# Operands of matmuls at multiples of 512 bytes from each other, and the inverse root spread by fp32r hi and lo products

## Chip, cores, metric

The kernel runs on one core of one Trainium2 chip. The metric is the device time of one execution in microseconds (us), here the median of three runs. TensorE is called PE, VectorE DVE, ScalarE ACT, GpSimd POOL; PEld stands for PE's weight loads, which overlap its matmuls.

## The reference

A trunk of two layers over 1024 tokens of width 1024, in fp32. Layer 0 mixes tokens by one projection that feeds stick-breaking attention (8 heads of 64) and a gated linear recurrence (4 heads of 128), and one output projection; layer 1 by a convolution module (gated projection, causal depthwise convolution of 31 taps, layer norm, projection). After each follows an MLP with squared ReLU, and each part has an RMS norm ahead and a residual.

```
for layer in range(DEPTH):
    u = rmsnorm(h, norm_mix_g[layer])
    if layer % 2 == 0:
        h = h + parallel_ab_mixer(u, w_in_ab[j], w_out_ab[j], lower_bounds[layer], hg_norm_g[j])
    else:
        h = h + conformer_conv(u, conv_w_glu[j], ...)
    u = rmsnorm(h, norm_ffn_g[layer])
    h = h + squared_relu_mlp(u, w_ff1[layer], w_ff2[layer])
return rmsnorm(h, final_norm_g)
```

## The kernel before

**Tiling.** Activations lie transposed, 128 channels on the partitions, and the tokens are worked in two halves of H = 512. A projection loops over panels of 128 output channels. `panel` loads one panel of weights (512 KB) over the SP queue into `wraw` and splits it into fp32r parts, `whl`: hi on ACT (line 99), lo on DVE (line 100). `gemm` (lines 110 to 112) then runs, for each 128 channels of the input, three matmuls: hi by hi, hi by lo, lo by hi. The panel's 128x128 block is the stationary operand, which PE loads ahead of each matmul, and the input (128x512, hi or lo) is the moving one. The input is split in the same way: tiles `u` (normed input), `ou` (output of the mixer), `cu` (convolution) and `hid` (hidden layer of the MLP). An MLP pass of one half does 8 hidden panels from `u`, then 8 output panels from these 8 `hid`, four times over; at the end of the kernel the last 8 output panels are done for 256 tokens at a time, four of their panels kept in `w2` tiles.

**Places in memory.** Pools lie one behind the other in a partition, and a tile's place is the sum of what stands ahead of it. Worked out from the built program, modulo 512 bytes: `wraw`, `whl`, `u`, `ou`, `cu` and `hx` lie at 96; the tiles of the working pool `wk` (attention and recurrence) at 128 (`kl`, `vn`), 192 (`raw`, `kd`, `qs`, `ke`, most `vh`) or 0 (`wt`, `kn`, one `vh`). The hidden layer of the first MLP pass takes tiles of the pool `up`, as `u` does, at 96. When attention is done its pool is closed, and from then on `hid` tiles come from a pool `hid` of their own, at 288. The MLP's gemms then write PSUM tiles `mm2`, those from `u` and those from `hid` alike.

**The inverse root.** `stats` turns sums of squares into 1/sqrt, for 4 (at the very end 2) blocks of 128 tokens: `st` matmuls against ones (line 121), a scale on DVE (line 124, `st_m`), a power on POOL (line 126, `st_r`), one Newton step in three DVE steps (lines 128 to 130), and `stb` matmuls (line 133), which spread each column of `st_r` over all partitions by a product with the identity, both in fp32. ACT copies the result out (line 135). It is called 21 times.

**Order.** A scheduler with a timeline of its own places the instructions of each engine; `tc.high_priority` moves the lines under it forward. The layer-0 mixer (to about 655 us) interleaves projection panels with attention and recurrence by hand-written spans; after that PE runs gemms almost alone.

Of the kernel before, what the change touches and what calls it, by code (L numbers as in the profile page):

```python
# [8 lines left out]
F32 = mybir.dt.float32  # L9
F32R = mybir.dt.float32r  # L10
BF16 = mybir.dt.bfloat16
AF = mybir.ActivationFunctionType
ALU = mybir.AluOpType
PSUM = bass.MemoryType.PSUM

P = 128
D = 1024
T = 1024
H = 512
# [34 lines left out]
def kernel(  # L54
# [13 lines left out]
    PE, ACT, DVE, POOL = nc.tensor, nc.scalar, nc.vector, nc.gpsimd  # L68

    const = ctx.enter_context(tc.tile_pool(name="const", bufs=1))  # L70
# [3 lines left out]
    tp = ctx.enter_context(tc.tile_pool(name="tp", bufs=2))  # L74
# [4 lines left out]
    nc.scalar.dma_start(vec, vecs)  # L79
    ident = const.tile([P, P], F32, name="ident")  # L80
    make_identity(nc, ident)
    ones = const.tile([P, P], F32, name="ones")
    DVE.memset(ones, 1.0)
    nhalf = const.tile([P, 4], F32, name="nhalf")
    POOL.memset(nhalf, -0.5)

    o_dram = [tc.dram_tile([P, T], F32, name=f"o_dram{i}") for i in range(KT)]

# [25 lines left out]
    def stats(pool, tag, src, count, eps, dst):  # L114

        n = dst.shape[-1] // P
        with tc.high_priority(offset=SPRIO):
            ps = pool.tile([P, H], F32, tag=tag, name="st")
            for c in range(n):
                for i, x in enumerate(src):  # L120
                    PE.matmul(ps[:, 2 * c:2 * c + 2], x[:, c * P:(c + 1) * P], ones[:, 0:2],  # L121
                              start=i == 0, stop=i == len(src) - 1, skip_group_check=True)
            m = tp.tile([P, 4], F32, tag="st_m", name="st_m")[:, :n]
            DVE.tensor_scalar(m, ps[:, 0:2 * n:2], 1.0 / count, eps, ALU.mult, ALU.add)
            r = tp.tile([P, 4], F32, tag="st_r", name="st_r")[:, :n]
            POOL.tensor_tensor(r, m, nhalf[:, :n], ALU.pow)
            t = tp.tile([P, 4], F32, tag="st_t", name="st_t")[:, :n]
            DVE.tensor_tensor(t, r, r, ALU.mult)
            DVE.scalar_tensor_tensor(t, t, -0.5, m, ALU.mult, ALU.mult)
            DVE.scalar_tensor_tensor(r, t, 1.5, r, ALU.add, ALU.mult)  # L130
            pb = pool.tile([P, H], F32, tag=tag, name="stb")
            for c in range(n):
                PE.matmul(pb[:, c * P:(c + 1) * P], r[:, c:c + 1].broadcast_to([P, P]), ident,  # L133
                          start=True, stop=True, skip_group_check=True)
            ACT.activation(dst, pb[:, :n * P], AF.Copy)

    def colsum_sq(src, w=H, order=range(KT), two=False):

        acc = tp.tile([P, H], F32, tag="acc", name="acc", bufs=1)[:, :w]
        for i, k in enumerate(order):  # L140
            x = src(k)
            if i == 0:
                ACT.activation(acc, x, AF.Square)
            else:
                sq = tp.tile([P, H], F32, tag="sq", name="sq")[:, :w]
                ACT.activation(sq, x, AF.Square)
                if not two or i < KT - 1:
                    DVE.tensor_tensor(acc, acc, sq, ALU.add)
        return [acc, sq] if two else [acc]

    def split(t, x):

        ACT.activation(t[:, 0], x, AF.Copy)
        DVE.tensor_tensor(t[:, 1], x, t[:, 0].bitcast(F32), ALU.subtract)  # L154

    def utile(name):
        return up.tile([P, 2, H], F32R, tag="u", name=name)

    def parts(ts):
        return [(t[:, 0], t[:, 1]) for t in ts]  # L160
# [13 lines left out]


    s1 = ctx.enter_context(ExitStack())
    wk = s1.enter_context(tc.tile_pool(name="wk", bufs=1))
    pz = s1.enter_context(tc.tile_pool(name="pz", bufs=2, space=PSUM))


# [34 lines left out]
    rm0 = wk.tile([P, H], F32, tag="rm0", name="rm0")  # L215
    with tc.high_priority(offset=PRIO):
        stats(pz, "tr", colsum_sq(lambda k: xs[0][k], two=True), D, 1e-6, rm0)

    def norm1():

        rm1 = wk.tile([P, H], F32, tag="ot", name="rm1", bufs=2)
        stats(pz, "tr", colsum_sq(lambda k: xs[1][k], two=True), D, 1e-6, rm1)
        u0[1] = scaled(lambda k: xs[1][k], V_MIX, rm1)
# [2 lines left out]
    lg = vec[:, V_LB:V_LB + 12].rearrange("p (r h) -> p r h", r=3)  # L226
    lb = const.tile([P, 4], F32, name="lb")
    lbc = const.tile([P, 4], F32, name="lbc")
    mx = wk.tile([P, 4], F32, name="lbmx")
    ex = wk.tile([P, 3, 4], F32, name="lbex")  # L230
    DVE.tensor_tensor(mx, lg[:, 0], lg[:, 1], ALU.max)
    DVE.tensor_tensor(mx, mx, lg[:, 2], ALU.max)
    for r in range(3):
# [46 lines left out]

    kl = [wk.tile([P, T], F32R, name=f"kl{h}") for h in range(2)]
    POOL.memset(kl[0][64:128].bitcast(F32), 0.0)
    POOL.memset(kl[1][0:64].bitcast(F32), 0.0)
    qs, kd, vn, vh, vl = {}, {}, {}, {}, {}
# [139 lines left out]
    def hg(hd, hf, dst):  # L427
# [95 lines left out]
        def output():  # L523
            qd, iv, before = hin[hd, "q", hf], hin[hd, "i", hf], L["before"]
            av = pz.tile([P, 4, P], F32, tag="av", name="ho")
            for c in range(4):
                PE.matmul(av[:, c], iv[:, c], L["sT"][:, c], start=True, stop=before[c] is None)
                if before[c] is not None:
                    PE.matmul(av[:, c], before[c], qd[:, c * P:(c + 1) * P], start=False, stop=True)
            L["av"] = av.rearrange("p c q -> p (c q)")  # L530
            sq = tp.tile([P, H], F32, tag="sq", name="hsq")
            ACT.activation(sq, L["av"], AF.Square)
            L["rh"] = wk.tile([P, H], F32, tag="ot", name="hrh", bufs=2)
            stats(pz, "tr", [sq], P, 1e-6, L["rh"])
# [73 lines left out]
    def rt():  # L608
        return late[0].tile([P, H], F32, tag="rbc", name="rbc", bufs=2)
# [75 lines left out]
    for name in TOKENS.split():  # L685
        f, n = name[0], name[1:]
# [14 lines left out]
        else:  # L701
            f, n, hf = name[:-2], int(name[-2]), "ab".index(name[-1])
# [53 lines left out]
    def ln_silu(ys):  # L756
        acc = tp.tile([P, H], F32, tag="acc", name="lacc", bufs=1)
        DVE.tensor_tensor(acc, ys[0], ys[1], ALU.add)
        for c in range(2, KT):
            DVE.tensor_tensor(acc, acc, ys[c], ALU.add)  # L760
        ps = pm2.tile([P, H], F32, tag="st", name="mean")
        PE.matmul(ps, ones, acc, start=True, stop=True)
        mu = tp.tile([P, H], F32, tag="sq", name="mu")
        ACT.activation(mu, ps, AF.Copy, scale=1.0 / D)
        for c in range(KT):
            DVE.tensor_tensor(ys[c], ys[c], mu, ALU.subtract)
        r = rt()
        stats(pm2, "st", colsum_sq(lambda c: ys[c]), D, 1e-5, r)
        res = []
        for c in range(KT):  # L770
            DVE.tensor_tensor(ys[c], ys[c], r, ALU.mult)
            DVE.tensor_scalar(ys[c], ys[c], vec[:, V_LNG + c:V_LNG + c + 1],
                              vec[:, V_LNB + c:V_LNB + c + 1], ALU.mult, ALU.add)
            sg = tp.tile([P, H], F32, tag="sq", name="sg")
            ACT.activation(sg, ys[c], AF.Sigmoid)
            DVE.tensor_tensor(sg, ys[c], sg, ALU.mult)
            res.append(utile("cu"))
            split(res[c], sg)
        return parts(res)
# [43 lines left out]
    steps(m, 8)  # L823
    ys = glu_conv(0, ug, m, 0)
    cu = ln_silu(ys)
    steps(m)
    ug = norm(1, V_MIX + 8)
    pw(cu, 0)
    ua = mlp_norm(1, 0)
    m = mlp(1, 0, ua)  # L830
    ys = glu_conv(1, ug, m, 3)
    cu = ln_silu(ys)
    steps(m, 24)
    pw(cu, 1)
# [66 lines left out]
```

## Time and profile before

| what | value |
|---|---|
| median of 3 runs | 2318.27 us (2317.86 to 2318.32) |
| profiled execution | 2317.94 us, its span 2316.2 us |
| PE busy | 2287.0 us (99%), 10828 matmuls |
| PEld, DVE, ACT, POOL busy | 1901.5, 1508.4, 884.9, 77.4 us |
| mean granted TensorE clock | 0.994 |

Busy time counts an instruction from its start to its end, and matmuls overlap; the pace of PE is read from starts. [...]

### The profile page before, as it was taken

Reading aid. Unit: us, or ns where it says so; the run is one execution under the profiler, and the core shown is the slowest. Engines: PE = TensorE matmul, PEld = TensorE weight load, DVE = VectorE, ACT = ScalarE, POOL = GpSimd, SP = SyncE. Lnnn points to the kernel's source line nnn. Section 1 sums busy time; section 2 is a strip of 40 time slices with the busy share of each in tenths; the row PEclk is TensorE's granted clock in tenths of the full one; section 3 lists DMA queues with packets and bytes.
Section 4 is the critical chain, followed back from the end, with each engine's and each line's share of the span. In section 5 each row is a group of like instructions: output and inputs, shape, how many; then the busy total and the mean of one; then the engine's idle time right before and its main releaser. Section 6 shows DMA issues by size and latency. Waiting matters only on the chain.

```text
span 2316.2 us, 27425 instructions
## 1 busy us (share of the span) xinstructions
PE 2287.0 (99%) x10828; PEld 1901.5 (82%) x10828; DVE 1508.4 (65%) x2156; ACT 884.9 (38%) x1338; POOL 77.4 (3%) x145
## 2 busy tenths in 40 slices
PE   8999999999999999999999999999999999999998
PEld 7888887788888888888888888888888888888888
DVE  7777777657443443469999866799997546333344
ACT  6444344434342333342414353341424534342341
POOL 1110000100000000000000000000000000000000
PEclk9999999999999999999999999999999999999999
DMA  4221122232333333323332322232322323323241
GB/s 171 69 67 44 49 69 62 89 125 86 111 128 103 94 98 95 96 91 96 96 98 93 96 95 91 91 100 91 100 91 91 100 97 104 117 91 100 91 137 46
DMA packets 67345, 217.97 MB, mean 94 GB/s; under 512 B 7696, under 2 KB 9872, under 8 KB 67216
## 3 DMA queue, kind: packets, MB, share of 16 engines
q1 hardware_dynamic: 55296, 197.16, 26.6%
q10 hardware_dynamic: 10640, 16.96, 2.3%
q0 software_dynamic: 1280, 2.10, 0.5%
q8 instruction: 85, 1.39, 0.2%
q14 instruction: 44, 0.36, 0.0%
HBM read 205.70 MB, written 8.39 MB: 92 GB/s over the span
## 4 chain that ended last, share of the span: by engine, by line
PE 93%; issue 3%; DVE 2%; DMA 1%; POOL 0%; ACT 0%; POOLq 0%; DVEq 0%; ACTq 0%
PE mm L110 26%; PE mm L111 26%; PE mm L112 26%; PE av L374 1%; PE pa L110 1%; PE pg L111 1%; PE pg L110 1%; PE pa L111 1%; PE pa L112 1%; PE pg L112 1%; PE wtr L365 1%; PE zs L466 1%; PE stb L133 1%; PE st L121 1%; PE z L345 1%
## 5 line engine op out<-in xcount | busy, mean ns | idle before, releaser
L100 DVE TENSOR_TENSOR whl<-wraw,whl 128x1024 fp32r<-128x1024 f32 x364 | 445.5, 1224 | 325.3 <-ACT whl L99 324.4
L99 ACT ACTIVATE whl<-wraw 128x1024 fp32r<-128x1024 f32 x364 | 384.5, 1057 | 695.8 <-PE mm L112 548.2
L110 PE MATMUL mm<-u,whl 128*128 128x512 f32 x1456 | 572.7, 394 | 8.3 <-ACT u L212 7.0
L111 PE MATMUL mm<-u,whl 128*128 128x512 f32 x1456 | 571.6, 393 | 1.4 <-DVE u L154 0.8
L112 PE MATMUL mm<-u,whl 128*128 128x512 f32 x1456 | 570.8, 392 | 0.0
L110 PE MATMUL mm<-hid,whl 128*128 128x512 f32 (+1 forms) x1024 | 396.8, 388 | 0.0
L111 PE MATMUL mm<-hid,whl 128*128 128x512 f32 (+1 forms) x1024 | 396.3, 387 | 0.0
L112 PE MATMUL mm<-hid,whl 128*128 128x512 f32 (+1 forms) x1024 | 396.1, 387 | 0.0
L753 DVE SCALAR_TENSOR_TENSOR y<-a,vec,y 128x512 f32<-128x512 f32 x480 | 345.0, 748 | 4.2
L110 PEld LDWEIGHTS mm<-u,whl 128*128 128x128 f32 x1456 | 274.0, 188 | 64.2 <-ACT u L212 7.0
L111 PEld LDWEIGHTS mm<-u,whl 128*128 128x128 f32 x1456 | 273.9, 188 | 56.1 <-DVE u L213 1.0
L112 PEld LDWEIGHTS mm<-u,whl 128*128 128x128 f32 x1456 | 274.0, 188 | 55.2 <-issue 0.2
L112 PEld LDWEIGHTS mm<-hid,whl 128*128 128x128 f32 x1024 | 191.9, 187 | 43.8
L111 PEld LDWEIGHTS mm<-hid,whl 128*128 128x128 f32 x1024 | 191.8, 187 | 43.7 <-issue 0.2
L110 PEld LDWEIGHTS mm<-hid,whl 128*128 128x128 f32 x1024 | 191.8, 187 | 43.5 <-issue 0.2
L654 DVE TENSOR_TENSOR ht<-ht,mm 128x512 f32<-128x512 f32 x120 | 82.5, 688 | 216.0 <-PE mm L112 215.6
L636 ACT ACTIVATE relu<-mm 128x512 f32<-128x512 f32 x128 | 76.5, 598 | 340.1 <-PE mm L112 331.6
L352 DVE TENSOR_TENSOR_SCAN ke<-ke 128x128 f32<-128x128 f32 (+5 forms) x64 | 86.3, 1352 | 23.6 <-POOL ke L349 23.0
L639 DVE TENSOR_TENSOR hid<-sqr,hid 128x512 fp32r<-128x512 f32 x128 | 87.9, 687 | 12.4 <-ACT sqr L638 12.4
L637 ACT ACTIVATE hid<-relu 128x512 fp32r<-128x512 f32 x128 | 79.6, 622 | 0.2
L638 ACT ACTIVATE sqr<-relu 128x512 f32<-128x512 f32 x128 | 79.5, 621 | 0.0
L374 PE MATMUL av<-wt,vh 128*128 128x256 f32 (+1 forms) x320 | 63.0, 295 | 4.5 <-DVE wt L370 3.7
(202 smaller groups left out, 2442.4 us busy)
## 6 DMA issues: line engine op xcount, KB each, us to landing
wraw<-w_ff SPq DMA_DIRECT2D x257, 512.0 KB, 3.5
wraw<-w_in SPq DMA_DIRECT2D x47, 512.0 KB, 3.6
wraw<-w_glu SPq DMA_DIRECT2D x32, 512.0 KB, 3.5
wraw<-w_out SPq DMA_DIRECT2D x16, 512.0 KB, 3.5
wraw<-w_pw SPq DMA_DIRECT2D x16, 512.0 KB, 3.5
xk<-xT SPq DMA_DIRECT2D x16, 256.0 KB, 5.4
oraw<-o_dram ACTq DMA_DIRECT2D x16, 256.0 KB, 2.8
ht<-xT ACTq DMA_DIRECT2D x16, 256.0 KB, 3.7
```

Of the source, the lines that this page charges most:

```text
L99: ACT.activation(hi[:, :n], raw[:, :n], AF.Copy)
L100: DVE.tensor_tensor(lo[:, :n], raw[:, :n], hi[:, :n].bitcast(F32), ALU.subtract)
L110: PE.matmul(ps, whi[:, c], hi, start=start and k == 0, stop=False)
L111: PE.matmul(ps, whi[:, c], lo, start=False, stop=False)
L112: PE.matmul(ps, wlo[:, c], hi, start=False, stop=stop and k == n - 1)
L352: DVE.tensor_tensor_scan(kr, kr, kr, 1.0, ALU.mult, ALU.min)
L374: PE.matmul(live["av"][:, qo + o:qo + 256], vh[hd, (b0 + b) // 4][:, (b0 + b) % 4, :], wt[:, part, b * 256:b * 256 + 256 - o], start=start ...
L637: ACT.activation(hh[:, 0], t, AF.Square)
L638: ACT.activation(s, t, AF.Square)
L639: DVE.tensor_tensor(hh[:, 1], s, hh[:, 0].bitcast(F32), ALU.subtract)
L654: DVE.tensor_tensor(d, d, ps, ALU.add)
L753: DVE.scalar_tensor_tensor(y, a[:, j:j + H], w(j), y, ALU.mult, ALU.add)
```

## The change

It moves every buffer that matmuls read so that they lie at multiples of 512 bytes from each other: `ones` shrinks from 128 columns to 2 (the matmul for the mean broadcasts one of them), fillers named `align` stand in two pools, and the working pool takes its large tiles first, in one list. In the built program `wraw`, `whl`, `u`, `ou`, `cu`, `hid` (early and late), `w2`, `kd`, `kl`, `qs`, `vh`, `wt`, `ke` and `kn` then all lie at 0 modulo 512; `acc` and `sq` at 256, the new `identr` at 64. And `stats` splits the inverse root into fp32r hi and lo (two more DVE steps) and spreads it by two fp32r matmuls for each block instead of one fp32 matmul.

```diff
-    ones = const.tile([P, P], F32, name="ones")
+    ones = const.tile([P, 2], F32, name="ones")
...
+    identr = const.tile([P, P], F32R, name="identr")
+    ACT.activation(identr, ident, AF.Copy)
+
+    const.tile([P, 96], F32, name="align")
...
             DVE.scalar_tensor_tensor(r, t, 1.5, r, ALU.add, ALU.mult)
+            rr = tp.tile([P, 2, 4], F32R, tag="st_rr", name="st_rr")[:, :, :n]
+            DVE.tensor_copy(rr[:, 0], r)
+            DVE.tensor_tensor(rr[:, 1], r, rr[:, 0].bitcast(F32), ALU.subtract)
             pb = pool.tile([P, H], F32, tag=tag, name="stb")
             for c in range(n):
-                PE.matmul(pb[:, c * P:(c + 1) * P], r[:, c:c + 1].broadcast_to([P, P]), ident,
-                          start=True, stop=True, skip_group_check=True)
+                for i in range(2):
+                    PE.matmul(pb[:, c * P:(c + 1) * P], rr[:, i, c:c + 1].broadcast_to([P, P]), identr,
+                              start=i == 0, stop=i == 1, skip_group_check=True)
...
+    tp.tile([P, 64], F32, tag="align", name="align", bufs=1)
     wk = s1.enter_context(tc.tile_pool(name="wk", bufs=1))
+
+    for tag, n, bufs, dt in (("rm0", H, 1, F32), ("raw", H, 2, F32), ("ot", H, 2, F32), ("vn", T, 1, F32),
+                             ("kd", T, 3, F32R), ("qs", H, 3, F32R), ("vh0", H, 2, F32R), ("vh1", H, 1, F32R),
+                             ("ke", T, 3, F32), ("wt", T, 2, F32R), ("kn", H, 1, F32)):
+        wk.tile([P, n], dt, tag=tag, name=tag, bufs=bufs)
+
+    kl = [wk.tile([P, T], F32R, name=f"kl{h}") for h in range(2)]
...
-    mx = wk.tile([P, 4], F32, name="lbmx")
-    ex = wk.tile([P, 3, 4], F32, name="lbex")
+    mx = wk.tile([P, 4], F32, tag="tot", name="lbmx")
+    ex = wk.tile([P, 3, 4], F32, tag="rtot", name="lbex")
...
-        PE.matmul(ps, ones, acc, start=True, stop=True)
+        PE.matmul(ps, ones[:, 0:1].broadcast_to([P, P]), acc, start=True, stop=True)
```

The change also moves instructions. PE in a late stage, around a `stb` group of a norm among the gemms of the next MLP. Before:

```order
3959 L112 MATMUL mm_8033<-u,whl 128x512
3960 L110 MATMUL mm_8033<-u,whl 128x512
3961 L133 MATMUL stb<-ident,st_r 128x128 x4
3962 L111 MATMUL mm_8033<-u,whl 128x512
3963 L112 MATMUL mm_8033<-u,whl 128x512
```

And of the change (lines 115 to 117 are the gemm, 142 `stb`):

```order
3969 L115 MATMUL mm_8139<-u,whl 128x512
3970 L116 MATMUL mm_8139<-u,whl 128x512
3971 L142 MATMUL stb<-identr,st_rr 128x128 x8
3972 L117 MATMUL mm_8139<-u,whl 128x512
3973 L115 MATMUL mm_8139<-u,whl 128x512
```

The group stands one gemm matmul later behind its `st`, and has eight matmuls in the program instead of four (each fp32 one runs as two passes).

PE in the mixer, where the last projection panels have ended and attention (`z`, `wtr`, `av`) goes on without them, from about 448 us of the trace. Before:

```order
1730 L112 MATMUL mm<-u,whl 128x512
1731 L133 MATMUL stb<-ident,st_r 128x128 x4
1732 L365 MATMUL wtr<-ident,ke 128x128 x3
1733 L275 MATMUL mm<-ident,dv 128x128 x4
1734 L365 MATMUL wtr<-ident,ke 128x128
1735 L345 MATMUL z<-kd,qs 128x256
1736 L346 MATMUL z<-kl_224,qs 128x256
1737 L374 MATMUL av<-wt,vh 128x256
```

And of the change (380 is `wtr`, 292 the turned values, 360 and 361 `z`, 389 `av`):

```order
1741 L117 MATMUL mm<-u,whl 128x512
1742 L142 MATMUL stb<-identr,st_rr 128x128
1743 L380 MATMUL wtr<-ident,ke 128x128 x3
1744 L142 MATMUL stb<-identr,st_rr 128x128 x7
1745 L360 MATMUL z<-kd,qs 128x256
1746 L361 MATMUL z<-kl_113,qs 128x256
1747 L292 MATMUL mm<-ident,dv 128x128 x4
1748 L389 MATMUL av<-wt,vh 128x256
```

The transposes now stand between the first `stb` matmul (hi) and the other seven, and the turned values behind a `z`. In the rows after these, too, the order differs.

DVE at the end of the kernel, the last inverse root and the final scaling. Before:

```order
1684 L124 TENSOR_SCALAR st_m<-st 128x2
1685 L128 TENSOR_TENSOR st_t<-st_r 128x2
1686 L129 SCALAR_TENSOR_TENSOR st_t<-st_t,st_m 128x2
1687 L130 SCALAR_TENSOR_TENSOR st_r<-st_t,st_r 128x2
1688 L792 SCALAR_TENSOR_TENSOR ht<-ht,vec,rbc 128x256 x8
```

And of the change:

```order
1735 L129 TENSOR_SCALAR st_m<-st 128x2
1736 L133 TENSOR_TENSOR st_t<-st_r 128x2
1737 L134 SCALAR_TENSOR_TENSOR st_t<-st_t,st_m 128x2
1738 L135 SCALAR_TENSOR_TENSOR st_r<-st_t,st_r 128x2
1739 L137 CAST st_rr<-st_r 128x2
1740 L138 TENSOR_TENSOR st_rr<-st_r,st_rr 128x2
1741 L807 SCALAR_TENSOR_TENSOR ht<-ht,vec,rbc 128x256 x8
```

The cast and the subtraction stand between the Newton step and the final scaling, with no other work of DVE there.

## Rows read from the trace of the kernel before

**Rows 1.** The page: busy us of each engine with its share and number of instructions, and the shares of the chain that ended last by engine.

```profile
PE 2287.0 (99%) x10828; PEld 1901.5 (82%) x10828; DVE 1508.4 (65%) x2156; ACT 884.9 (38%) x1338; POOL 77.4 (3%) x145
...
PE 93%; issue 3%; DVE 2%; DMA 1%; POOL 0%; ACT 0%; POOLq 0%; DVEq 0%; ACTq 0%
```

**Rows 2.** The view of waits of PE, longest in total first: who waited for whom, us in total, times, the longest.

```profile
PE mm L110 <- ACT u L212: 7.0, 1, 7.0
PE av L374 <- DVE wt L370: 3.7, 4, 2.2
...
PE stb L133 <- DVE st_r L130: 1.7, 1, 1.7
```

**Rows 3.** Windows (us from the span's start): length, busy us and number of instructions of PE, PEld, DVE, ACT and POOL, granted clock, DMA share, GB/s. PE runs hid against panels in the first (first MLP pass) and the third, u against panels in the others.

```profile
642.00:654.00 12.00, 12.00 (x54) 9.92 (x54) 5.31 (x7) 2.65 (x3) 0.12 (x1) 1.00 0.32 109
658.00:698.00 40.00, 40.00 (x178) 33.14 (x177) 18.11 (x22) 23.05 (x35) 0.00 (x0) 1.00 0.41 132
702.00:742.00 40.00, 40.00 (x173) 32.08 (x172) 14.94 (x16) 8.15 (x9) 0.00 (x0) 1.00 0.30 95
...
2127.00:2167.00 40.00, 40.00 (x178) 33.16 (x177) 13.61 (x15) 18.09 (x28) 0.00 (x0) 1.00 0.28 93
```

**Rows 4.** The timeline of PE: the first and the last matmul that the first three of these windows count. Columns: start us, us, engine, line, operation, tiles, shape.

```profile
641.82 0.40 PE L111 MATMUL mm<-hid,whl 128*128 128x512 f32 x1
...
653.84 0.39 PE L110 MATMUL mm<-hid,whl 128*128 128x512 f32 x1
...
657.69 0.39 PE L112 MATMUL mm<-u,whl 128*128 128x512 f32 x1
...
697.81 0.39 PE L112 MATMUL mm<-u,whl 128*128 128x512 f32 x1
...
701.73 0.39 PE L111 MATMUL mm<-hid,whl 128*128 128x512 f32 x1
...
741.87 0.39 PE L112 MATMUL mm<-hid,whl 128*128 128x512 f32 x1
```

**Rows 5.** Groups of instructions by line and shape: line, engine, operation, tiles, shape, count | busy us, mean ns of one | idle before. The first three count from 655.8 us on, the last is the page's, of the whole span.

```profile
L110 PE MATMUL mm<-hid,whl 128*128 128x512 f32 x896 | 353.4, 395 | 0.0
...
L110 PE MATMUL mm<-hid,whl 128*128 128x256 f32 x64 | 18.1, 283 | 0.0
...
L110 PE MATMUL mm<-hid,w 128*128 128x256 f32 x64 | 17.7, 281 | 0.0
...
L110 PE MATMUL mm<-u,whl 128*128 128x512 f32 x1456 | 572.7, 394 | 8.3 <-ACT u L212 7.0
```

**Rows 6.** The timeline of PE near the end, matmuls of 256 columns; three stand between the two.

```profile
2289.76 0.28 PE L110 MATMUL mm<-hid,w 128*128 128x256 f32 x1
...
2290.23 0.28 PE L111 MATMUL mm<-hid,w 128*128 128x256 f32 x1
```

**Rows 7.** The timeline of PE within the mixer (nine u matmuls stand between the first two), and of PEld in the same stretch, where two loads are merged in one row.

```profile
299.79 0.39 PE L110 MATMUL mm<-u,whl 128*128 128x512 f32 x1
...
302.06 0.39 PE L111 MATMUL mm<-u,whl 128*128 128x512 f32 x1
302.29 0.22 PE L345 MATMUL z<-kd,qs 128*128 128x128 f32 x1
302.35 0.28 PE L346 MATMUL z<-kl,qs 128*128 128x128 f32 x1
...
302.29 0.19 PEld L346 LDWEIGHTS z<-kl,qs 128*128 128x128 f32 x1
302.40 0.30 PEld L374 LDWEIGHTS av<-wt,vh 128*128 128x128 f32 x2
```

**Rows 8.** The timeline of PE in layer 1: a `stb` group, and the second and the eighth gemm matmul behind it.

```profile
1426.14 1.05 PE L133 MATMUL stb<-ident,st_r 128*128 128x128 f32 x8
...
1427.26 0.39 PE L112 MATMUL mm<-cu,whl 128*128 128x512 f32 x1
...
1428.65 0.39 PE L112 MATMUL mm<-cu,whl 128*128 128x512 f32 x1
```

**Rows 9.** Windows in the mixer, columns as in rows 3; the last counts PE's matmuls with panels (tile `whl`) alone, busy us and number, clock, DMA share, GB/s.

```profile
40.00:655.00 615.00, 603.45 (x3224) 514.53 (x3223) 437.81 (x713) 260.21 (x457) 50.22 (x97) 0.98 0.25 77
...
366.00:376.00 10.00, 9.32 (x41) 8.72 (x42) 9.22 (x15) 4.12 (x9) 0.76 (x2) 0.51 0.00 1
...
462.00:472.00 10.00, 9.50 (x42) 8.84 (x42) 5.54 (x14) 4.31 (x10) 0.58 (x2) 0.53 0.62 204
...
40.00:655.00 615.00, 453.43 (x1812) 0.98 0.25 77
```

**Rows 10.** The timeline of DVE at the end: the last two steps of the last inverse root.

```profile
2307.11 0.16 DVE L129 SCALAR_TENSOR_TENSOR st_t<-st_t,st_m 128x2 f32<-128x2 f32 x1
2307.30 0.16 DVE L130 SCALAR_TENSOR_TENSOR st_r<-st_t,st_r 128x2 f32<-128x2 f32 x1
```

**Rows 11.** The timeline of ACT at the start: its first activation, with the idle time ahead of it and what ended that.

```profile
5.25 1.06 ACT L99 ACTIVATE whl<-wraw 128x1024 fp32r<-128x1024 f32 x1 [2.71 <-DMA wraw<-w_in]
```

**Rows 12.** Ahead of the first layer norm: the timeline of DVE with the last sum for its mean, that of PE with the matmul of the mean, and the window that counts PE's matmuls on `hid` alone.

```profile
1307.63 0.69 DVE L760 TENSOR_TENSOR lacc<-lacc,y 128x512 f32<-128x512 f32 x1
...
1313.26 0.59 PE L762 MATMUL mean<-lacc,ones 128*128 128x512 f32 x1
...
1020.00:1313.00 293.00, 127.78 (x545) 1.00 0.31 96
```

More of the change, by code (lines that the diff above doesn't have):

```diff
@@ L277, in proj @@
         return raw
-    kl = [wk.tile([P, T], F32R, name=f"kl{h}") for h in range(2)]
     POOL.memset(kl[0][64:128].bitcast(F32), 0.0)
```

## The prediction

> **What bounds the kernel now.** I read the page first: TensorE (PE) is busy 99% of the 2316.2 us and the chain that ended last lies on it for 93% [rows 1]. The view of waits then shows how little PE waits for anybody: 7.0 us once at the start, and after that nothing over 3.7 us in total [rows 2]. So a change pays here if it alters how fast matmuls follow each other, or makes PE wait. Busy time cannot show the first, because matmuls overlap (0.39 us each, started every 0.23 us). I therefore took starts, from the timeline at both ends of stretches that hold one kind of matmul alone, and their count from the windows [rows 3, 4]; a window also counts the matmul that is still running at its left edge, so 178 matmuls are 177 steps.
>
> - u against w panels, 657.69 to 697.81 us: 177 steps in 40.12 us, **226.7 ns** a matmul. The window of 40 us from 2127 us holds 178 too.
> - hid against w panels, 701.73 to 741.87 us: 172 steps in 40.14 us, **233.4 ns**.
> - hid in the first MLP pass (642 us): 53 steps from 641.82 to 653.84, 12.02 us, **226.8 ns**.
>
> [...] The two kinds of hid differ in one thing that I can find: early hid tiles come from the pool `up` and lie at 96 modulo 512 like the panels, late ones come from the pool `hid` and lie at 288, 192 bytes off. The late u matmuls write the same PSUM tiles (`mm2`) as late hid, so PSUM is not the difference.
>
> **The change part by part.**
>
> *Late hid matmuls.* From 655.8 us on line 110 issues 896 hid matmuls of 512 columns [rows 5], and lines 111 and 112 as many each: 2,688. In the changed kernel hid and panels both lie at 0. If the distance is what counts, each goes from 233.4 to 226.7: 2,688 x 6.7 ns = **-18.0 us**. All of it is on the path, since PE is busy without a gap in these windows [rows 3].
>
> [...]
>
> *hid matmuls of 256 columns* (two kinds of panel, 64 on each of three lines, 384 [rows 5]) start 0.47 us / 4 = 117.5 ns apart [rows 6]. No row has them aligned. Bounds: 0, or the full 6.7 ns, 2.6 us in all. Two weight loads take 0.30 us from the first's start to the second's end, and one takes 0.19, so they follow each other at 0.11 [rows 7]. At 117.5 little is left above that: I take 0.
>
> *Attention stage (40 to 655 us).* The u matmuls there are at 226.7 already when undisturbed: 299.79 to 302.06 is 10 steps in 2.27 us [rows 7]. What becomes aligned are the small ones (kd, kl, qs, vh, wt) and the edges between them and u. The matmuls after an interruption run unevenly: 1427.26 to 1428.65 is 6 steps in 1.39 us, 232 ns [rows 8]. The stage has 3,224 matmuls, 1,812 of them with panels [rows 9]. Bounds: 0, and 6.7 ns on each of the other 1,412, 9.5 us. Most of those are too short to overlap a whole load as a 512-wide one does, so I stay near nothing: **-1.5 us**.
>
> *The inverse root by hi and lo.* A `stb` group issues 8 passes today: fp32 matmuls run as two passes each (160 in the trace for 80 in the program) and 8 take 1.05 us, (1.05 - 0.28)/7 = 110 ns apart [rows 8]. The change issues 8 fp32r matmuls with 8 weight loads. For 128 columns of fp32r the rows show 0.06 us from start to start once (302.29 to 302.35), but loads follow at 0.11 [rows 7]. Bounds: 160 x -50 ns = -8 us, or 0. A group of eight is paced by its loads, so I take **0**.
>
> *Two more DVE steps per inverse root* (cast, subtract). At the end the steps of 128x2 start 0.19 us apart [rows 10], so +0.38 us from `st_r` to `stb`. Twenty of the 21 groups are hidden by other matmuls placed between: the list of waits has one wait of PE for `st_r`, 1.7 us [rows 2], and that is the last group. Without that cover the steps would cost 0.38 us a group, 8 us in all. On DVE nothing urgent queues behind them. The last group is bare: **+0.4 us**; its four passes stay four.
>
> *Const and start.* The copy to `identr` stands first on ACT and waits for the select that makes `ident`, among POOL's first instructions. ACT sits idle for 2.71 us until 5.25, when the first panel lands [rows 11]; the copy lies in that. Nothing. The smaller `ones` and the padding move no work.
>
> *The order.* In the late stages `stb` only moves back by one gemm matmul. In the attention stage the scheduler puts many things elsewhere; the sparse stretch after 448 us is laid out anew. [...]
>
> *What is late next.* In the first convolution PE's pace rises and DVE's does not. DVE's sum for the mean ends at 1308.3 us and PE takes it at 1313.3 [rows 12]. 545 hid matmuls lie before that from 1020 us on [rows 12], 3.7 us by the new pace: the 5.0 us of slack shrink to 1.3 and hold.
>
> Sum: -18.0 - 1.5 + 0.4 = -19.1 us on the profiled execution's 2317.94 us, 2298.8. The median shown is 0.33 us above that execution: **2299.1 us**.
>
> **The rivals.**
>
> [...]
>
> *Slower: the place itself counts, not the distance.* No row has a 512-wide matmul with both operands at 0. If 0 and 0 is as bad as 288 and 96, late hid gains nothing and the u matmuls alone, 1,456 on each of three lines [rows 5], go from 226.7 to 233.4: 4,368 x 6.7 ns = +29 us, 2318.3 + 29 + 0.4 = 2348. It decides from 19.1 us / 4,368 = 4.4 ns a u matmul on, if late hid does gain. For it: the kernel has no row that excludes it. Against it: the rows vary the distance and the pace follows; nothing in them singles out a place.
>
> *The attention stage eats it.* The new order opens three more half-clock stretches with waits of their own (3 x 5 us plus 4 us): 2318 again. For it: two such stretches exist, and one of them (462 us) lies in the part that is laid out anew. Against it: the order around the first is unchanged, and all waits there make 11.6 us.
>
> **How the numbers follow.** Forecast case 0.85, at 2289 to 2308: 2299.1 with +-6 for the order; on the low side part of the attention bound (8 us more), the 2.6 us of 256 columns and part of the 8 us of `stb`; on the high side the order and a pace gain that comes only in part. No effect 0.06, slower by place 0.04, attention eats it 0.03, still faster than the range 0.02. The range 2289 to 2308 leaves out less than 2 in 10. Runs of this kernel tell 0.2%, 4.6 us, from no change. Faster: 0.85 + 0.02 and a bit of the rest, 0.88; same: 0.07; slower: 0.05.
>
> **What would show it.** Windows on late hid with 177 or 178 matmuls in 40 us instead of 173; windows on u still with 178; eight `stb` in 1.0 to 1.1 us; the last `stb` 0.4 us later after its `st_m`; half-clock stretches before 655 us counted again. I am wrong if late hid stays at 173, or if u falls to 173.

## The result, and the profile after

The changed kernel takes **2301.51 us** (median of 4 runs, 2300.16 to 2305.74), the kernel before beside it on the same chip 2318.07 us: ratio **0.9932 [0.9915, 0.9949]**, or 16.6 us less. That is faster, as forecast, 2.4 us above the 2299.1 and inside the range. The profiled execution is the slowest of the four, 2305.74 us with a span of 2304.0; why it is slow is part of the story below.

The page of the changed kernel: busy us of each engine, and the chain that ended last by engine. It is still PE's kernel, as in [rows 1]:

```profile
PE 2273.3 (99%) x10828; PEld 1906.4 (83%) x10828; DVE 1513.3 (66%) x2198; ACT 886.3 (38%) x1339; POOL 78.5 (3%) x145
...
PE 93%; issue 4%; DVE 2%; ACT 1%; DMA 0%; POOL 0%; POOLq 0%; DVEq 0%; ACTq 0%
```

The stretches of [rows 3] again, in the trace of the change (PE, PEld, DVE, ACT, POOL busy and number, granted clock, DMA share, GB/s). The first runs early hid, the second u, the third late hid, the fourth u again:

```profile
642.00:654.00 12.00, 12.00 (x59) 10.06 (x58) 5.26 (x6) 2.72 (x3) 0.12 (x1) 1.00 0.30 89
662.00:702.00 40.00, 40.00 (x179) 33.10 (x177) 17.47 (x21) 22.64 (x34) 0.00 (x0) 1.00 0.39 133
706.00:746.00 40.00, 40.00 (x179) 33.10 (x178) 15.21 (x16) 9.41 (x10) 0.00 (x0) 1.00 0.33 103
2114.00:2154.00 40.00, 40.00 (x178) 33.14 (x177) 13.21 (x15) 18.49 (x29) 0.00 (x0) 1.00 0.29 93
```

Late hid holds 178 or 179 matmuls in 40 us where it held 173, at the same clock of 1.00; u holds 178 as ever. From the starts of the 192 late hid matmuls of that pass, one takes 226.66 ns, and the later passes run at the same pace, a few matmuls behind an interruption aside.

Next, where the time went. The same work can be cut out of both traces: from the last matmul on `u` in the mixer, where the sparse stretch begins, 316 PE matmuls on (to 514.08 us before), from there to the first matmul of 256 columns, and from there to the last one. Windows of PE (length, busy us and number, granted clock, DMA share, GB/s; a count differs by one or two, since a window also counts what is still running at its left edge and a few records are missing). Of the kernel before:

```profile
448.20:514.08 65.88, 61.83 (x318) 0.92 0.41 132
514.08:2257.48 1743.40, 1743.40 (x7757) 1.00 0.31 99
2257.48:2303.77 46.29, 46.29 (x396) 1.00 0.11 38
```

Of the changed kernel:

```profile
448.74:518.91 70.17, 65.47 (x317) 0.88 0.38 124
518.91:2244.30 1725.39, 1725.20 (x7756) 1.00 0.32 100
2244.30:2291.57 47.27, 47.27 (x396) 1.00 0.11 37
```

Up to the cut the change is 0.5 us late (448.74 for 448.20), in the sparse stretch it loses 4.3 us, in the long middle it gains **18.0 us**, in the 256 columns it loses **1.0 us**, and what is left to the end takes 12.5 us in either. Together -12.2 us, the difference of the two spans (2304.0 and 2316.2). The granted clock of 0.88 for 0.92 in the first row belongs to the loss there. These are the half-clock stretches before 655 us in the change, to be held against [rows 9], which has two (columns as in the first of these groups, PE alone):

```profile
363.00:375.00 12.00, 11.22 (x54) 0.57 0.05 12
441.00:447.00 6.00, 5.16 (x16) 0.72 0.12 25
459.00:470.00 11.00, 10.51 (x49) 0.53 0.45 160
476.00:484.00 8.00, 7.00 (x22) 0.57 0.37 121
```

In the trace's record of the clock a granted 0.50 (half-clock) lasts 10.2 us twice before, and 10.2, 3.4, 10.2 and 6.8 us after. PE's waits over the whole run (who waited for whom, us in total, times, longest) are a little longer than [rows 2]:

```profile
PE av L389 <- DVE wt L385: 3.9, 4, 2.2
...
PE mm L115 <- DVE qs L335: 2.0, 1, 2.0
PE stb L142 <- DVE st_rr L137: 1.9, 1, 1.9
PE ho L544 <- DVE state L533: 1.7, 2, 1.4
```

### The profile page after: what moved, and what is told of

The parts are those of the page before. It is cut to its first block, busy times and chain, and to the rows that moved or that the text cites. A ratio compares the mean times of both kernels' runs of the same rounds, so it can differ in the third digit from the quotient of the medians.

```text
span 2304.0 us, 27457 instructions
## 1 busy us (share of the span) xinstructions
PE 2273.3 (99%) x10828; PEld 1906.4 (83%) x10828; DVE 1513.3 (66%) x2198; ACT 886.3 (38%) x1339; POOL 78.5 (3%) x145
## 3 DMA queue, kind: packets, MB, share of 16 engines
q8 instruction: 85, 1.39, 0.2%
## 4 chain that ended last, share of the span: by engine, by line
PE 93%; issue 4%; DVE 2%; ACT 1%; DMA 0%; POOL 0%; POOLq 0%; DVEq 0%; ACTq 0%
PE mm L115 26%; PE mm L117 26%; PE mm L116 26%; PE av L389 1%; PE pa L115 1%; PE pg L115 1%; PE pg L116 1%; PE pa L117 1%; PE pa L116 1%; PE pg L117 1%; PE wtr L380 1%; PE zs L481 1%; PE st L126 1%; PE stb L142 1%; DVE ke L367 1%
## 5 line engine op out<-in xcount | busy, mean ns | idle before, releaser
L115 PE MATMUL mm<-hid,whl 128*128 128x512 f32 (+1 forms) x1024 | 392.5, 384 | 0.0
L116 PE MATMUL mm<-hid,whl 128*128 128x512 f32 (+1 forms) x1024 | 391.9, 383 | 0.0
L117 PE MATMUL mm<-hid,whl 128*128 128x512 f32 (+1 forms) x1024 | 391.6, 383 | 0.0
L117 PEld LDWEIGHTS mm<-hid,whl 128*128 128x128 f32 x1024 | 192.5, 188 | 37.4
```

The source lines that it names most:

```text
L115: PE.matmul(ps, whi[:, c], hi, start=start and k == 0, stop=False)
L116: PE.matmul(ps, whi[:, c], lo, start=False, stop=False)
L117: PE.matmul(ps, wlo[:, c], hi, start=False, stop=stop and k == n - 1)
```

## Experiments

The theory to test: the distance between the moving operand (`hid`) and the panel sets how fast 512-column matmuls follow each other, and the rest of the change moves a few microseconds. The rivals: the place itself counts; or something else in the change did it, the new root for one. In each kernel below, "places" are the fillers, the shorter `ones` and the list of tiles; "root" is the spreading by hi and lo.

### Places alone

```diff
-            DVE.tensor_copy(rr[:, 0], r)
-            DVE.tensor_tensor(rr[:, 1], r, rr[:, 0].bitcast(F32), ALU.subtract)
...
-                for i in range(2):
-                    PE.matmul(pb[:, c * P:(c + 1) * P], rr[:, i, c:c + 1].broadcast_to([P, P]), identr,
-                              start=i == 0, stop=i == 1, skip_group_check=True)
+                PE.matmul(pb[:, c * P:(c + 1) * P], r[:, c:c + 1].broadcast_to([P, P]), ident,
+                          start=True, stop=True, skip_group_check=True)
```

(against the changed kernel; the tiles of the new root stay as fillers, so every place is the change's and the order of every engine is that of before).

> The places of the changed kernel with the inverse root as before; every engine has the instructions of the kernel before in its order, so only addresses differ. Theory (distance between moving and stationary operand sets the pace, the order is worth nothing by itself): late hid at 226.7 ns, 2318.1 - 18.0 - 1.5 = 2298.6 us, ratio 0.9916, half-clock stretches two as before. Rival (part of the gain comes from the new order or the new stb): 2318.1 less only a part, above 2304 us.

Measured: 2298.05 us (2297.79 to 2298.86, 4 runs), ratio 0.9920 [0.9906, 0.9935], a span of 2296.6. Late hid in its first pass, and the three cuts of above (windows of PE):

```profile
699.00:739.00 40.00, 40.00 (x178) 1.00 0.32 97
...
446.17:512.04 65.87, 61.85 (x318) 0.92 0.41 132
512.04:2237.11 1725.07, 1725.07 (x7757) 1.00 0.32 100
2237.11:2284.38 47.27, 47.27 (x396) 1.00 0.12 38
```

The places give the whole 18.3 us of the middle and the loss of 1.0 us at 256 columns, and the sparse stretch takes what it took before (65.87 for 65.88). Up to it this kernel is 2.0 us earlier (446.17 for 448.20), with the same half-clock time ahead of it (10.2 us in both); more than half of that is there at 38 us already and is not the places' doing (the part on the attention stage below). The change as a whole is no faster than its first half.

### Root alone

```diff
+    identr = const.tile([P, P], F32R, name="identr")
+    ACT.activation(identr, ident, AF.Copy)
...
+    tp.tile([P, 112], F32, tag="align", name="align", bufs=1)
```

(with the new lines of `stats`, against the kernel before; the filler keeps panels at 96 and late hid at 288, and the order is that of the change).

> The inverse root of the changed kernel with the places of the one before (fillers keep panels at 96 and late hid at 288); every engine has the changed kernel's order. Theory: +0.4 us at the end, late hid stays at 233.4 ns, and the new order of the mixer is what is left; the changed kernel lies 2.4 us above its forecast, so 2318.5 to 2322 us, ratio 1.000 to 1.002, with the third half-clock stretch in some runs. Rival (the eight fp32r matmuls are cheaper than eight fp32 passes): 2310 us.

Measured: 2318.71 us (2317.58 to 2321.18, 10 runs), ratio 1.0012 [1.0003, 1.0022], which is 0.7 to 5.1 us more than before. Late hid, and the sparse stretch:

```profile
702.00:742.00 40.00, 40.00 (x173) 1.00 0.34 103
...
445.85:515.09 69.24, 63.08 (x317) 0.93 0.40 126
```

Late hid stays at 173, so the root has no part in the gain. The sparse stretch takes 3.4 us more than before with the same matmuls: PE sits idle 6.2 us of it (69.24 - 63.08) instead of 4.1 (65.88 - 61.83).

### Every operand shifted by 96 bytes

```diff
-    const.tile([P, 96], F32, name="align")
+    const.tile([P, 96 + 24], F32, name="align")
```

> The changed kernel with 96 bytes more of filler in the first pool: all operands lie at 96 instead of 0 modulo 512, still at multiples of 512 from each other, order unchanged. Theory (distance): u and hid at 226.7 ns, the time of the changed kernel within 3 us, 2298 to 2304. Rival (the place itself counts): u and hid move off 226.7 ns; 1 ns on 8,832 matmuls of 512 columns is 9 us.

Measured: 2303.11 us (2301.3 to 2304.87, 4 runs), ratio 0.9942 [0.9927, 0.9956]. Late hid, and the sparse stretch, in the order of the change:

```profile
702.00:742.00 40.00, 40.00 (x178) 1.00 0.33 100
...
445.57:514.40 68.83, 62.64 (x317) 0.93 0.40 127
```

With all operands at 96 modulo 512 the pace of late hid is as good as with all at 0, and u holds 179 matmuls in the 40 us from 658. In these runs the distance counts, not the place.

### Fourteen distances

```diff
+                        o = DIST[passes[0]] // 4
+                        hh = late[1].tile([P, 2 * H + P], F32R, tag="hid", name="hid")[:, o:o + 2 * H].rearrange(
+                            "p (a b) -> p a b", a=2)
...
+    DIST = [0, 16, 32, 48, 64, 96, 128, 160, 192, 256, 320, 384, 448, 496, 192]
```

(the changed kernel with 8 buffers of `hid` instead of 9, each 512 bytes longer; every late pass of the MLP puts its hid at another distance from the panels; the last entry is the pass of 256 columns).

> The changed kernel with the hid tiles of the 15 late MLP passes at 0, 16, 32, 48, 64, 96, 128, 160, 192, 256, 320, 384, 448, 496 and (256 columns) 192 bytes modulo 512 from the panels, eight buffers instead of nine; order unchanged. Theory A (the two streams meet once wherever they start apart): 226.7 ns at 0 and 233.3 at every other distance, and the 256-column pass at 117.8 ns as before instead of the 120.0 of the changed kernel. Rival B (the cost grows with the distance): near 226.7 at 16 and 496, most at 256. Rival C (only some distances cost): paces between, a distance with less than 226.7 ns not excluded.

Measured: a single run, 2312.74 us. Windows inside the passes at 32, 128 and 192 (40 us), and at 256, 320 and 384 (24 us):

```profile
920.00:960.00 40.00, 40.00 (x173) 1.00 0.31 93
1364.00:1404.00 40.00, 40.00 (x173) 1.00 0.32 99
1676.00:1716.00 40.00, 40.00 (x173) 1.00 0.30 92
1785.00:1809.00 24.00, 24.00 (x107) 1.00 0.34 97
...
1913.00:1937.00 24.00, 24.00 (x106) 1.00 0.33 102
1990.00:2014.00 24.00, 24.00 (x104) 1.00 0.29 90
```

The mean of the last 20 steps of each pass, worked out from starts:

| distance modulo 512, bytes | ns a matmul |
|---|---|
| 0, 256 | 226.65, 226.70 |
| 64, 320 | 228.85, 229.05 |
| 16 | 231.65 |
| 32, 48, 96, 128, 160, 192 | 233.35, 233.35, 233.45, 233.35, 234.0, 233.3 |
| 384, 448, 496 | 233.3, 233.35, 233.35 |

A distance of 256 is as good as 0, and 320 as good as 64; 128 and 384, and 192 and 448, lie within 0.05 ns of each other too: in this run the pattern repeats after 256 bytes. Most other distances cost 6.7 ns, but 64 only 2.2 and 16 only 5.0, so it is not a plain "aligned or not". 192 and 448, the mirror of 64, cost the full price. No distance was under 226.65. So the third theory holds: only some distances cost, and not in proportion. The pass of 256 columns, at 192, took 45.76 us.

### The last pass at 192

The kernel before has its 256-column matmuls at 192, and they are faster there; the run with many distances showed the same. So the places-only kernel was run with the hid of that one pass put back out of step (as in the run before, the pool `hid` has 8 buffers instead of 9, each 512 bytes longer):

```diff
-                        hh = late[1].tile([P, 2, H], F32R, tag="hid", name="hid")
+                        o = 48 if last is not None and f0 == FT - GF else 0
+                        hh = late[1].tile([P, 2 * H + P], F32R, tag="hid", name="hid")[:, o:o + 2 * H].rearrange(
+                            "p (a b) -> p a b", a=2)
```

> The changed places with the old inverse root, as in the places-only kernel (2298 us, 0.992 of before), but the hid tiles of the very last MLP pass, the one whose matmuls have 256 columns, lie 192 bytes modulo 512 from their panels instead of 0. Theory A (a matmul of 256 columns is the faster the other way round: the rows had 120.0 to 120.5 ns aligned, 117.8 at 192 in the kernel before, 116.6 in the run with many distances): the 383 steps of that pass take 1 to 1.6 us less than in the places-only kernel, about 44.8 instead of 46.2 us, nothing else changes, and the time is 2296.5. Rival B (the 116.6 came from the passes before it, which were out of step too): the pass stays at 120 ns and the time at 2298.

Measured: 2297.90 us (2296.68 to 2298.38, 5 runs), ratio 0.9918 [0.9904, 0.9932]. The pass of 256 columns:

```profile
2237.41:2283.71 46.30, 46.30 (x396) 1.00 0.12 39
```

46.30 us for the 47.27 aligned, as in the kernel before (46.29), and the middle takes the 1725.07 us of the places alone. The 1.0 us is there in the trace and back with one offset; against the places-only kernel's 2298.05 and 2298.39 the medians cannot tell it. The gain is at the lower end of what was expected, and the two lengths expected for the pass were each 1 us or more too low.

The run with many distances has no single pace of 116.6 ns in this pass but two, and the root-alone kernel, at 192 too, has the same two (its pass takes 45.87 us). The mean step in three stretches of the pass between interruptions, worked out from starts (other matmuls, `st` and `stb`, stand behind steps 200, 218 and some 256 to 260):

| kernel | steps 1 to 195 | 222 to 255, behind `st` | 263 to 383, behind `stb` |
|---|---|---|---|
| before, last pass at 192 | 117.8 ns | 113.7 | 117.8 |
| root alone (192) | 117.8 | 117.8 | 113.5 |
| fourteen distances (192) | 117.8 | 113.7 | 113.4 |
| the change, places alone (0) | 120.0 | 119.8 | 120.0 |

So at 192 the pace goes from one level to another behind an interruption (117.8 and 113.4 to 113.7 ns), and the distance alone does not set it; at 0 it hardly moves (119.8 to 120.0). Which interruption leaves which pace is open.

### Eight distances within the last pass

```diff
-                        o = 48 if last is not None and f0 == FT - GF else 0
+                        o = DIST[f - f0] // 4 if last is not None and f0 == FT - GF else 0
...
+    DIST = [0, 32, 64, 96, 128, 192, 224, 256]
```

> As the run with the last pass at 192, but the eight hid tiles of that pass lie at 0, 32, 64, 96, 128, 192, 224 and 256 bytes modulo 512 from their panels. If the pace of 256 columns goes by the distance of each matmul (theory A), matmuls on the tiles at 0 and 256 step by about 120 ns and those at 96 to 192 by 113 to 118. If the pace belongs to the pass as a whole or to the time since its start (rival B), all eight have one pace within 1 ns. Time near 2297 to 2298.

Measured: a single run, 2298.7 us. The timeline of PE: three matmuls on the tile at 192 and the first at 224, then three at 0 and the first at 32 (start us, us, engine, line, tiles, shape):

```profile
2245.22 0.28 PE L114 MATMUL mm<-hid,w 128*128 128x256 f32 x1
2245.34 0.28 PE L115 MATMUL mm<-hid,w 128*128 128x256 f32 x1
2245.45 0.28 PE L116 MATMUL mm<-hid,w 128*128 128x256 f32 x1
2245.56 0.28 PE L114 MATMUL mm<-hid,w 128*128 128x256 f32 x1
...
2246.27 0.28 PE L114 MATMUL mm<-hid,w 128*128 128x256 f32 x1
2246.39 0.28 PE L115 MATMUL mm<-hid,w 128*128 128x256 f32 x1
2246.51 0.28 PE L116 MATMUL mm<-hid,w 128*128 128x256 f32 x1
2246.63 0.28 PE L114 MATMUL mm<-hid,w 128*128 128x256 f32 x1
```

Three steps take 0.34 us at 192 and 0.36 us at 0. Over the pass the steps within a tile, those at interruptions left out, have means of 113.8 ns at 192, 117.1 at 224, and 118.5 to 119.5 at the other six. The pace goes by the tile, as the first theory says, but 96 and 128, at 119.2 and 119.1 ns, gain next to nothing, and only 192 and 224 do. The tile at 192 steps at about the lower of the two paces of the table above; why at that one is open.

### The new root in the late stages only

```diff
+            if late:
+                DVE.tensor_copy(rr[:, 0], r)
+                DVE.tensor_tensor(rr[:, 1], r, rr[:, 0].bitcast(F32), ALU.subtract)
...
+                if not late:
+                    PE.matmul(pb[:, c * P:(c + 1) * P], r[:, c:c + 1].broadcast_to([P, P]), ident,
+                              start=True, stop=True, skip_group_check=True)
+                for i in range(2 if late else 0):
```

(the changed kernel otherwise; the mixer's roots are the old ones, and the mixer is laid out in the order of before).

> The changed kernel with the new inverse root in the late stages only; up to 655 us each root is the old one, so that the attention stage is laid out in the order of before. Theory A (the new order of the attention stage is what the places-only kernel gains over the changed one): the sparse stretch, 1248th to 1270th gemm matmul, takes 32 us as before instead of 36 to 37.4, the late root costs 0 to 0.4 us, and the time is 2298 to 2299, the places-only kernel's. Rival B (the two more DVE steps and the loads of the root cost it in the late stages, a little each time): 2301 or more with a sparse stretch of 32 us.

Measured: 2298.99 us (2297.66 to 2300.99, 4 runs), ratio 0.9924 [0.9910, 0.9938], a span of 2296.8. The sparse stretch, and the middle, which holds most of the new roots:

```profile
446.22:511.78 65.56, 61.92 (x317) 0.92 0.42 133
511.78:2236.85 1725.07, 1725.07 (x7756) 1.00 0.33 100
```

The sparse stretch is back at its old length, and the middle is that of the places alone to the last digit. By the count of the expectation, 1248th to 1270th gemm matmul, the sparse stretch is 31.8 us, 32.1 before and 37.4 in the change. So the new root costs and gives nothing where gemms cover it (1725.07 us with it and without); what it costs, it costs in the mixer, apart from 0.2 us at the kernel's bare end (below). That it is the order there, and not the root's own instructions, is argued: PE waits nowhere in the sparse stretch for `st_rr`, but no run has the new order with the old root.

### Places alone, a second time

> The places-only kernel again, beside the other three on one chip: 2298 us, 0.992 of before; half-clock stretches before 655 us as in its first run (two of 10 us, 364 and 460 us). If the stretches change from run to run by chance, its sparse stretch differs from 32 us by some 5 us here too; if they belong to the order, it is 32 us again.

Measured: 2298.39 us (2298.24 to 2300.25, 4 runs), ratio 0.9923 [0.9909, 0.9937]. The two half-clock stretches are again 10.2 us each, at 364 and 460 us. The sparse stretch:

```profile
446.38:512.35 65.97, 61.74 (x317) 0.92 0.42 132
```

By the count of the expectation it is 32.2 us, as in the first run: the order, more than the run, sets its length.

All profiled executions together, the sparse stretch (316 matmuls): the old order in the mixer took 65.9, 65.9, 66.0, 65.9, 64.8 and 65.6 us (before, places alone twice, last pass at 192, eight distances, root late only), the new order 70.2, 69.2, 68.8 and 66.6 us (the change, root alone, shifted, fourteen distances). The two sets do not overlap: the old order is steady, the new one 0.7 to 4.3 us longer than before and uneven. Part of that goes with the half-clock time within the stretch. Where it is 10.2 us, the old order takes 65.6 to 66.0 us and the new one 68.8 and 69.2, some 3 us more; the new order's 66.6 us had 3.4 us of it and its 70.2 us had 17.1.

## Why the prediction was right, and where it was off

**Late hid, -18.0 us: right.** The middle shrank by 18.0 us in the change and 18.3 in the places alone, with 226.66 ns a matmul. In the run with fourteen distances one offset moves the pace of the same matmuls from 226.65 ns at 0 to 233.3 at 192. With that no effect, at 0.06 in the forecast, is out too: the place of the tiles, and nothing that was written into them, made late hid slow. Why the distance counts was not found; the runs give the pattern alone.

**u stays at 226.7, the rival of the place: right to hold it small.** The run with everything at 96 gives the same windows, 178 matmuls on late hid and 179 on u.

**Attention stage by alignment, -1.5 us: the right sign, but mis-sized, about twice too large.** The places alone reach the sparse stretch 1.8 to 2.0 us earlier than before (446.17, 446.38 and 446.44 for 448.20, the last of these with the last pass at 192; half-clock time ahead of it 10.2 us in all four). But 0.9 to 1.2 us of that is there at 38 us, where the same matmul starts at 38.02 us before and at 36.78, 37.12 and 37.02 in these three. At the start matmuls of 512 columns follow each other every 0.43 us and then every 0.23, from 14.0 us on before and from about 12 us on in these three. That is not the places' doing: the run with eight distances, the same program as these three up to its last pass, also changes pace only at 14.0 us and has this matmul at 37.78 us. From it to a matmul at about 300 us and on to the sparse stretch, before and in the places alone:

```profile
38.02:299.56 261.54, 259.95 (x1440) 1.00 0.20 58
299.56:448.20 148.64, 142.74 (x770) 0.97 0.23 69
```

```profile
36.78:297.81 261.03, 259.49 (x1441) 1.00 0.20 58
297.81:446.17 148.36, 142.49 (x769) 0.97 0.24 69
```

The first part, at full clock, is 0.5 us shorter in all five traces with these places and the old order. The second is 0.3 to 0.4 us shorter in the three of above, 0.1 with the root late only, and 0.4 longer with the eight distances, whose half-clock times differ. So 0.5 us are shown, and 0.8 to 0.9 at equal half-clock time, against one trace of before. Which of the small matmuls give it was not separated. The unevenness behind an interruption is not it: it is there with everything aligned. The timeline of PE in the change, around a `stb` group that answers to [rows 8]:

```profile
1422.13 1.00 PE L142 MATMUL stb<-identr,st_rr 128*128 128x128 f32 x8
...
1423.25 0.39 PE L115 MATMUL mm<-cu,whl 128*128 128x512 f32 x1
...
1424.64 0.39 PE L115 MATMUL mm<-cu,whl 128*128 128x512 f32 x1
```

Six steps in 1.39 us, to the digit what [rows 8] has.

**256 columns, 0 with a bound on the side of gain alone: the sign was wrong.** Aligned they follow each other at 120.0 ns, for 117.8 in most of the pass before, and the pass takes 1.0 us more. The bound was carried over from 512 columns, where aligned is faster; a loss was not even allowed for. A single pair of rows, as in [rows 6], sees one of the two paces that the pass has at 192 (the table above).

**stb, 0: right.** Eight take 1.00 us in the row above, for 1.05. The trace counts eight weight loads for a group in either kernel; the first two matmuls start 0.06 us apart for 0.11, and all other steps are 0.11 us in both.

**Const and start, 0: right.** The copy to `identr` starts on ACT at 2.60 us and takes 0.31; the first panel is there at 5.08.

**The tail, +0.4 us: +0.2, one step and not two.** The last root of the kernel, DVE, PE and ACT in their order of time (the first row answers to the second of [rows 10]):

```profile
2295.10 0.16 DVE L135 SCALAR_TENSOR_TENSOR st_r<-st_t,st_r 128x2 f32<-128x2 f32 x1
2295.30 0.17 DVE L137 CAST st_rr<-st_r 128x2 fp32r<-128x2 f32 x1
2295.50 0.16 DVE L138 TENSOR_TENSOR st_rr<-st_r,st_rr 128x2 fp32r<-128x2 f32 x1
...
2295.61 0.85 PE L142 MATMUL stb<-identr,st_rr 128*128 128x128 f32 x4 [1.91 <-DVE st_rr L137]
2296.50 0.38 ACT L144 ACTIVATE rbc<-stb 128x256 f32<-128x256 f32 x1 [3.68 <-PE stb L142]
```

PE starts at 2295.61, while the subtraction (L138) still runs: the first matmul is the hi one and needs only the cast, so one DVE step of 0.2 us lies on the path and not two. From the start of `st_m` to the first `stb` it is 1.86 us (2293.75 to 2295.61), and 1.67 before (2305.94 to 2307.61). From `st_m` to ACT's copy it is 2.75 us for 2.79 before, but that compares two clocks: the granted clock falls to 0.50 while the group runs and is 0.68 over the four matmuls here and 0.56 before, which then take 0.85 and 1.08 us. Where it is 1.00, they take 0.66 us with the new root (root alone) and 0.68 with the old one (last pass at 192), and from `st_m` to the copy it is 2.56 and 2.39 us.

**Slack in the convolution, 5.0 us to 1.3: it holds, but the working was wrong.** DVE's last sum and PE's matmul for the mean, as in [rows 12]:

```profile
1305.15 0.69 DVE L775 TENSOR_TENSOR lacc<-lacc,y 128x512 f32<-128x512 f32 x1
...
1310.50 1.02 PE L777 MATMUL mean<-lacc,ones 128*128 128x512 f32 x2
```

The slack is 4.7 us (1310.50 - 1305.84). DVE's sum ended 2.5 us earlier and PE's matmul came 2.8 us earlier, so DVE's sums are not a fixed pace that PE runs into. That they follow what PE hands DVE is a reading that no run tested.

**The order, 0 with 6 us to either side: this term was mis-sized.** It costs 0.7 to 4.3 us in the sparse stretch, always on the same side. The place was named (the part laid out anew), the mechanism in the rival as well (more half-clock stretches and waits). What failed is the mean of 0: in all four traces the new order is longer, by about 3 us at equal half-clock time. No run shows the 6 us to either side, nor the 5 us a stretch of the rival, half of the 10 us that [rows 9] have at 0.51 and 0.53: between the new order's 66.6 and 70.2 us lie 13.7 us more of half-clock time and 3.6 us more in length. The rows of the order gave a sign of it: `z` moved ahead of the turned values and the transposes between the first `stb` and the rest, in a stretch where PE already had 4.1 us idle in 65.88. In the stretch from `stb` to the first matmul on `ou`, PE in the root-alone kernel waits 2.0 us for `state`, 1.1 for `hf`, 1.1 for `ke` and 0.7 for `hsq`; the kernel before waits 1.4 for `ke`, 1.1 for `wt` and 0.7 for `hf` there. Which of the moves costs most was not separated. Why the length of the half-clock stretches varies from run to run, in either order, is open.

By medians and traces: -18.0 for late hid, -0.8 for the mixer's places, +1.0 for 256 columns and +0.2 for the tail make -17.6 us. Measured are -16.6, which leaves +1.0 for the order, inside what root alone costs by its own ratio (0.7 to 5.1 us). The forecast of -19.1 lies 2.5 us below the measured: the attention term was 0.7 too large, the 1.0 at 256 columns and the 1.0 of the order were missing, and the tail was 0.2 too dear. The large term, late hid, was right in mechanism and size, so this is not luck; all the misses together are a seventh of it.

## What to carry to other kernels

Read the pace of back-to-back matmuls from starts, not from busy time (here 0.39 us busy, and a start every 0.23), for each kind of tile; where the same shape runs at two paces, compare the addresses of the two operands and try the moving tiles at 0 or 256 bytes modulo 512 from the stationary ones with a filler. Here that gave 226.7 ns for 233.4 at 512 columns; at 256 columns 0 cost 1.0 us, and 256 stepped at 118.5 to 119.5 ns, as 0 did. Before a gain is read off two traces from their starts, compare the same matmul some 40 us in: here that point alone differed by up to 1.3 us. An edit that costs nothing by its instructions can still move a scheduler's order: where PE has waits and the granted clock already falls, price the new order there as a loss (here 0.7 to 4.3 us), or keep the old form of the code in that stretch. Half of this change was enough: the places alone, or the new root kept out of the mixer, are by their ratios 1.9 to 2.8 us faster than both together, though the intervals overlap; the sparse stretches of the traces say the same.

## What the runs showed of the hardware that was not expected

- At 512 columns the pattern repeats after 256 bytes, not 512, in the one run that tried it: 226.7 ns at 0 and 256, about 229 at 64 and 320, 231.7 at 16, 233.3 to 234.0 at the other nine distances tried.
- Matmuls of 256 columns go the other way: 120.0 ns aligned, and with all tiles at 192 either 117.8 or about 113.5, which in these traces changes only behind an interruption by other matmuls; 113.8 on a tile at 192 among tiles at other distances.
- Between 14 and 655 us the stretches at a granted clock of 0.50 lasted between 3.4 and 10.2 us, and the same instructions ahead of one do not settle its length: at 364 to 369 us it was 10.2 us in the run with the last pass at 192 and 6.8 us in the one with eight distances, two kernels that differ in nothing before the last pass.
